# Splitting the last load and the first store of one DMA queue into unequal rows

**Chip, cores, metric.** One core of a Trainium2 chip. The metric is the device time of one execution in microseconds (us).

## The reference

Rotary position embedding with scaled positions, on x of shape (8, 8, 1024, 64) in fp32, 16.8 MB in and 16.8 MB out:

```python
angles = np.outer(positions * scale, freqs)          # (1024, 32)
cos, sin = np.cos(angles), np.sin(angles)
x_first, x_second = x[..., :32], x[..., 32:]
out = concatenate([x_first*cos - x_second*sin, x_first*sin + x_second*cos], -1)
```

## The kernel before

x is cut into four units of 4 MB, 128 partitions of 32 KB each. GpSimd's DMA queue loads the units and casts them to fp16 on the way (half of unit 0 comes as fp32 over the two other queues). VectorE does four products and sums a half unit, ScalarE casts the result back to fp32. Units 0 and 1 are stored by the same GpSimd queue, units 2 and 3 by SyncE's, a half unit at a time.

```python
N = 8192; NH = 4096; NU = 4                     # columns of a unit, of half a unit; units
X  = [xin.tile([P, K, 2, half], FP16, name=f"X{u}") for u in range(NU)]
pin(nc.gpsimd.dma_start(out=Xf[0][:, :NH], in_=xv[0][:, :NH]))
# ... constants on GpSimd ...
for u in range(1, NU):
    pin(nc.gpsimd.dma_start(out=Xf[u], in_=xv[u]))           # fp32 -> fp16
# ... sine and cosine tables (T) ...
for u in range(NU):
    OUT = xout.tile([P, N], FP32, tag="O")
    for s in range(2):
        # pr = X*sin; X = X*cos; X0 = X0 - pr1; X1 = pr0 + X1     (VectorE, half a unit)
        pin(nc.scalar.copy(out=OUT[:, ns], in_=Xf[u][:, ns]))
        if u >= NU // 2:
            pin(nc.sync.dma_start(out=ov[u][:, ns], in_=OUT[:, ns]))
    if u < NU // 2:
        pin(nc.gpsimd.dma_start(out=ov[u], in_=OUT))
```

`pin` keeps the program order on each engine. The queue of GpSimd therefore holds: units 0 to 3 in, unit 0 out, unit 1 out.

Of the kernel before, what the change touches and what calls it, by code (L numbers as in the profile page):

```python
# [21 lines left out]
def kernel(  # L22
# [8 lines left out]
    nc = tc.nc  # L31
    pin = tc.keep_in_program_order
# [8 lines left out]
    N = K * D  # L41
    NU = NBH // HEADS
# [2 lines left out]
    K8 = S // P  # L45
    G = P // HP
    W = K8 * half
    assert S % HP == 0 and D == 2 * half and NBH % HEADS == 0 and G * K8 == K

    fscale = float(scale)  # L50

    xv = x.rearrange("b h s d -> (b h s d)").rearrange("(u p n) -> u p n", p=P, n=N)
    ov = out.rearrange("b h s d -> (b h s d)").rearrange("(u p n) -> u p n", p=P, n=N)
# [21 lines left out]
    Xf = [t.rearrange("p k h j -> p (k h j)") for t in X]  # L75
# [12 lines left out]
        out=one, in_=one, compare_op=ALU.not_equal, fill=1.0, base=0,  # L88
        pattern=[[-1, G], [-G, HP]], channel_multiplier=1,
    ))  # L90
    for u in range(1, NU):
        pin(nc.gpsimd.dma_start(out=Xf[u], in_=xv[u]))  # L92


    pin(nc.vector.tensor_copy(out=sel, in_=one.unsqueeze(2).broadcast_to((P, G, HEADS, HP))))  # L95
# [5 lines left out]
        out=posf, in_=pos_i64.bitcast(I32).rearrange("p (k t) -> p k t", t=2)[:, :, 0]  # L101
# [3 lines left out]
        out=y,  # L105
# [8 lines left out]
        out=r, in0=m, scalar=_MAGIC, in1=y, op0=ALU.subtract, op1=ALU.subtract  # L114
# [5 lines left out]
        out=ra.bitcast(I32), in0=r.bitcast(I32), scalar1=0x7FFFFFFF, scalar2=None, op0=ALU.bitwise_and  # L120
# [5 lines left out]
    for g in range(0, G, 2):  # L126
        ps = spread.tile([P, 2, 2, W], FP32, tag="g")
        for i in range(2):
            nc.tensor.matmul(  # L129
                out=ps[:, i].rearrange("p t w -> p (t w)"),  # L130
# [12 lines left out]
# [3 lines that stand above are left out]
            ks = slice(s * KH, (s + 1) * KH)  # L146
            ns = slice(s * NH, (s + 1) * NH)
            Xs = X[u][:, ks]
            sin_b = T[:, 0, ks].unsqueeze(2).broadcast_to((P, KH, 2, half))
            cos_b = T[:, 1, ks].unsqueeze(2).broadcast_to((P, KH, 2, half))  # L150
            pr = tmp.tile([P, KH, 2, half], FP16, tag="pr")
            pin(nc.vector.tensor_tensor(out=pr, in0=Xs, in1=sin_b, op=ALU.mult))  # L152
            pin(nc.vector.tensor_tensor(out=Xs, in0=Xs, in1=cos_b, op=ALU.mult))  # L153
            pin(nc.vector.tensor_tensor(  # L154
                out=Xs[:, :, 0, :], in0=Xs[:, :, 0, :], in1=pr[:, :, 1, :], op=ALU.subtract
            ))
            pin(nc.vector.tensor_tensor(  # L157
                out=Xs[:, :, 1, :], in0=pr[:, :, 0, :], in1=Xs[:, :, 1, :], op=ALU.add
            ))
            pin(nc.scalar.copy(out=OUT[:, ns], in_=Xf[u][:, ns]))  # L160
            if u >= NU // 2:
                pin(nc.sync.dma_start(out=ov[u][:, ns], in_=OUT[:, ns]))
        if u < NU // 2:
            pin(nc.gpsimd.dma_start(out=ov[u], in_=OUT))  # L164


# [33 lines left out]
```

## Time and profile before

| | before |
|---|---|
| time, median of the runs given with the change | 84.56 us (84.42 to 84.83) |
| span in the profile | 82.8 us |
| HBM traffic over the span | 406 GB/s |
| VectorE / ScalarE busy | 73% / 49% |
| last ScalarE copy ends / last DMA packet ends | 73.4 / 81.5 us |

The last row is the one to start from: computing is over 8 us before the transfers are. The profile's own lines are shown in the prediction.

A word on how the text counts. Sixteen DMA engines share each transfer; each has 8 of the 128 rows. The profile records each row that an engine moves as a packet, with its start and duration; "packet records" below means these. From the start of one 32 KB row of fp32 to the start of the next, an engine takes 1.21 us, loaded or stored. Durations of single rows come out some 0.01 to 0.02 us longer.

### The profile page before, as it was taken

To read this page: it belongs to the slowest core of one execution; us is meant where nothing else is said; L and a number is where in the kernel's file an instruction comes from. 1 tells how busy PE (TensorE), PEld (TensorE's weight loads), DVE (VectorE), ACT (ScalarE), POOL (GpSimd) and SP (SyncE) were. 2 spreads that over 40 slices of the span, in tenths; PEclk is the share of its full clock that TensorE was granted. 3 is DMA by queue.
4 is the path that set the end of the run, shared out by engine and by line. 5 is a ranking of instruction groups with operands and counts; after the bars stand their busy time and mean duration, and the time that the engine had idled before them with its cause. 6 is when DMAs were issued, how large, how long until landed. Compare 5 with 4: busy or idle time off the path is not lost.

```text
span 82.8 us, 179 instructions
## 1 busy us (share of the span) xinstructions
PE 7.0 (8%) x18; PEld 2.7 (3%) x18; DVE 60.3 (73%) x40; ACT 40.1 (49%) x18; POOL 4.6 (6%) x14
## 2 busy tenths in 40 slices
PE   0011799200000000000000000000000000000000
PEld 0011233000000000000000000000000000000000
DVE  0306276999999999999999999999999997000000
ACT  0602159999960690294088049209606912950000
POOL 4920000000000002000000200000000000000000
PEclk9999999975555555555555555555555555555555
DMA  2899998997999899699979989999899999999991
GB/s 40 335 326 269 293 333 182 253 238 150 246 253 198 182 253 238 143 253 253 127 301 459 507 348 412 507 443 420 380 436 420 412 420 436 444 420 436 428 428 55
DMA packets 1874, 26.22 MB, mean 317 GB/s; under 512 B 338, under 2 KB 338, under 8 KB 338
## 3 DMA queue, kind: packets, MB, share of 16 engines
q0 software_dynamic: 864, 15.73, 66.4%
q1 hardware_dynamic: 720, 9.44, 27.2%
q10 hardware_dynamic: 290, 1.06, 3.2%
HBM read 16.79 MB, written 16.78 MB: 406 GB/s over the span
## 4 chain that ended last, share of the span: by engine, by line
DVE 55%; ACT 14%; issue 6%; DMA 6%; PE 5%; DVEq 1%; ACTq 0%
DVE pr L152 19%; DVE X L153 19%; DVE X L157 9%; DVE X L154 6%; DMA freq_row<-in_freqs_dram 6%; ACT T L139 5%; ACT OUT L160 4%; PE ps L129 4%; ACT X L140 4%; DVEq L195 1%; PE cfreq L97 1%; ACT tab L122 1%; DVE r L113 1%; DVE y L104 1%; ACTq L69 0%
## 5 line engine op out<-in xcount | busy, mean ns | idle before, releaser
L160 ACT CAST OUT<-X 128x4096 f32<-128x4096 f16 x8 | 28.8, 3606 | 24.2 <-DVE X L157 24.2
L152 DVE TENSOR_TENSOR pr<-X,T 128x4096 f16<-128x4096 f16 x8 | 18.3, 2292 | 1.0 <-ACT T L139 0.7
L153 DVE TENSOR_TENSOR X<-X,T 128x4096 f16<-128x4096 f16 x8 | 18.3, 2292 | 0.3
L154 DVE TENSOR_TENSOR X<-X,pr 128x2048 f16<-128x2048 f16 x8 | 9.8, 1225 | 0.3
L157 DVE TENSOR_TENSOR X<-pr,X 128x2048 f16<-128x2048 f16 x8 | 9.7, 1219 | 0.0
L139 ACT CAST T<-ps 128x1024 f16<-128x1024 f32 x6 | 5.7, 1030 | 2.6 <-PE ps L129 2.6
L129 PE MATMUL ps<-tab,sel 128*128 128x512 f16 x16 | 6.4, 584 | 2.2 <-ACT tab L122 2.2
L137 DVE CAST T<-ps 128x1024 f16<-128x1024 f32 x2 | 2.5, 1225 | 2.2 <-PE ps L129 2.2
L140 ACT CAST X<-X0f 128x4096 f16<-128x4096 f32 x1 | 3.7, 3651 | 0.0
L164 POOL DMA_DIRECT2D out_dram<-OUT x2 | 1.1, 536 | 40.3 <-ACT OUT L160 40.3
L95 DVE COPY sel<-one 128x2048 f16<-128x2048 f16 x1 | 0.7, 693 | 2.8 <-POOL one L87 2.8
L117 ACT ACTIVATE tab<-r 128x256 f16<-128x256 f32 x1 | 0.4, 416 | 4.3 <-DVE r L113 4.3
L129 PEld LDWEIGHTS <-sel 128*128 128x128 f16 x16 | 2.2, 138 | 6.0 <-issue 5.8
L117 ACT ACT_TABLE_LOAD x1 | 1.3, 1283 | 2.1 <-issue 2.1
L92 POOL DMA_DIRECT2D X<-in_x_dram x3 | 2.0, 658 | 0.0
L100 DVE CAST posf<-pos_i 128x8 f32<-128x8 int32 x1 | 0.2, 172 | 2.3 <-DMA pos_i<-in_positions_dram 2.3
L97 PE MATMUL cfreq<-freq_row,coef 1*128 1x32 f32 x2 | 0.6, 392 | 5.9 <-DMA freq_row<-in_freqs_dram 5.9
L104 DVE TENSOR_TENSOR y<-posf,cfreq 128x256 f32<-128x256 f32 x1 | 0.4, 422 | 0.5 <-PE cfreq L97 0.5
L83 POOL DMA_DIRECT2D X<-in_x_dram x1 | 0.7, 667 | 0.8 <-POOLq L181 0.8
L97 PEld LDWEIGHTS cfreq<-freq_row,coef 1*128 1x128 f32 x2 | 0.5, 305 | 5.8 <-issue 5.8
L122 ACT ACTIVATE tab<-ra,quarter 128x256 f16<-128x256 f32 x1 | 0.5, 507 | 0.0
L113 DVE SCALAR_TENSOR_TENSOR r<-m,y 128x256 f32<-128x256 f32 x1 | 0.4, 424 | 0.0
(10 smaller groups left out, 1.9 us busy)
## 6 DMA issues: line engine op xcount, KB each, us to landing
out_dram<-OUT POOLq DMA_DIRECT2D x2, 4096.0 KB, 20.8
out_dram<-OUT SPq DMA_DIRECT2D x4, 2048.0 KB, 11.6
X<-in_x_dram POOLq DMA_DIRECT2D x3, 2048.0 KB, 28.7
X0f<-in_x_dram SPq DMA_DIRECT2D x1, 1024.0 KB, 4.8
X<-in_x_dram POOLq DMA_DIRECT2D x1, 1024.0 KB, 11.7
X0f<-in_x_dram ACTq DMA_DIRECT2D x1, 1024.0 KB, 12.2
pos_i<-in_positions_dram ACTq DMA_DIRECT2D x1, 8.0 KB, 5.0
freq_row<-in_freqs_dram ACTq DMA_DIRECT2D x1, 0.1 KB
```

The source lines that it names most:

```text
L92: pin(nc.gpsimd.dma_start(out=Xf[u], in_=xv[u]))
L97: nc.tensor.matmul(out=cfreq, lhsT=coef, rhs=freq_row, start=True, stop=True)
L117: pin(nc.scalar.activation(out=tab[:, 0], in_=r, func=AF.Sin, bias=0.0, scale=-_TWO_PI_DN))
L129: nc.tensor.matmul(out=ps[:, i].rearrange("p t w -> p (t w)"), lhsT=sel[:, g + i].rearrange("s h q -> s (h q)"), rhs=tab.rearrange("s t k ...
L137: pin(nc.vector.tensor_copy(out=dst, in_=ps))
L139: pin(nc.scalar.copy(out=dst, in_=ps))
L140: pin(nc.scalar.copy(out=Xf[0][:, NH:], in_=X0f[:, :NH]))
L152: pin(nc.vector.tensor_tensor(out=pr, in0=Xs, in1=sin_b, op=ALU.mult))
L153: pin(nc.vector.tensor_tensor(out=Xs, in0=Xs, in1=cos_b, op=ALU.mult))
L154: pin(nc.vector.tensor_tensor(out=Xs[:, :, 0, :], in0=Xs[:, :, 0, :], in1=pr[:, :, 1, :], op=ALU.subtract))
L157: pin(nc.vector.tensor_tensor(out=Xs[:, :, 1, :], in0=pr[:, :, 0, :], in1=Xs[:, :, 1, :], op=ALU.add))
L160: pin(nc.scalar.copy(out=OUT[:, ns], in_=Xf[u][:, ns]))
```

## The change

Its intent: at the point where the queue of GpSimd goes from loads to stores, make the rows small, so that whatever is lost there is lost on small rows.

```diff
+    C1 = 512
+    C2 = 1024
...
     for u in range(1, NU):
-        pin(nc.gpsimd.dma_start(out=Xf[u], in_=xv[u]))
+        c = C2 if u == NU - 1 else 0
+        pin(nc.gpsimd.dma_start(out=Xf[u][:, : N - c], in_=xv[u][:, : N - c]))
+        if c:
+            pin(nc.gpsimd.dma_start(out=Xf[u][:, N - c :], in_=xv[u][:, N - c :]))
...
         if u < NU // 2:
-            pin(nc.gpsimd.dma_start(out=ov[u], in_=OUT))
+            c = C1 if u == 0 else 0
+            if c:
+                pin(nc.gpsimd.dma_start(out=ov[u][:, :c], in_=OUT[:, :c]))
+            pin(nc.gpsimd.dma_start(out=ov[u][:, c:], in_=OUT[:, c:]))
```

## The prediction

> **What bounds the kernel now.** I first asked whether an engine or the transfers bound it. The page's head and the slices answer, with the number of bytes:
>
> ```profile
> PE 7.0 (8%) x18; PEld 2.7 (3%) x18; DVE 60.3 (73%) x40; ACT 40.1 (49%) x18; POOL 4.6 (6%) x14
> ...
> DMA  2899998997999899699979989999899999999991
> ...
> HBM read 16.79 MB, written 16.78 MB: 406 GB/s over the span
> ```
>
> VectorE is busy 73% of the span and ScalarE 49%, while the DMA row is at 8 or 9 nearly everywhere (its single 6s and 7s come from packets being counted in the slice where they start; all sixteen engines step almost together). The second row of the page that matters is the chain, and it is a trap here: it is made of VectorE pieces and ends with the last ScalarE copy,
>
> ```profile
> 67.45 1.22 DVE X L154
> 68.67 1.15 DVEq L195
> 69.82 0.02 issue
> 69.84 3.60 ACT OUT L160
> ```
>
> that is at 73.44 us, but the span is 82.8 us. After it only the last 2 MB store is issued (73.47 us in the timeline). The packet records of the trace show that its packets don't start then: the last eight rounds of 16 KB packets on the SyncE queue start at 76.64 us and end at 81.50. So the last store waits some 3 us behind its own queue. The compute chain has those 3 us of slack, less the time from issue to a first packet (about 1 us for the first load of all, issued at 0.74, first packet at 1.75), so about 2 us. The bound is the sum of the transfers. Check: 33.57 MB at the 430 GB/s of the last stretch below is 78.1 us; from the first packet at 1.75 us that gives 79.8, and the packets end at 81.5. About 1.7 us are lost somewhere, and that is all that any re-cutting of transfers can win.
>
> Next I looked for where they are lost. I put the edges of windows on the starts of rounds of packets (one row a DMA engine, sixteen engines):
>
> ```profile
> core 0: us, PE busy (x) PEld busy (x) DVE busy (x) ACT busy (x) POOL busy (x), PEclk, DMA share, GB/s
> 21.88:31.57 9.69, 0.00 (x0) 0.00 (x0) 9.55 (x6) 5.74 (x2) 0.05 (x1) 0.50 1.02 216
> 31.57:38.82 7.25, 0.00 (x0) 0.00 (x0) 7.15 (x5) 3.61 (x1) 0.49 (x1) 0.50 1.02 217
> 38.82:42.03 3.21, 0.00 (x0) 0.00 (x0) 3.15 (x4) 0.38 (x1) 0.00 (x0) 0.50 1.06 163
> 42.03:51.73 9.70, 0.00 (x0) 0.00 (x0) 9.56 (x6) 6.26 (x2) 0.53 (x1) 0.50 1.00 433
> ...
> 66.29:80.88 14.59, 0.00 (x0) 0.00 (x0) 3.49 (x3) 3.76 (x2) 0.00 (x0) 0.50 1.00 430
> ```
>
> The last column counts bytes written, and a load casts fp32 to fp16, so 217 GB/s there is 434 GB/s read: loads and stores run at one pace, 32 KB of fp32 in 1.21 us an engine. Only the third line falls out: the last two rows of unit 3 (2 x 16 x 16 KB = 524 KB) take 3.21 us, where 217 GB/s would give 2.42. That is 0.8 us lost, with the engines busy all the time (share 1.06): the packets themselves are slow. Their records say so: every load row took 1.23 us; of the last two, the first took 1.23 to 1.71 us and the second 1.81 to 2.17. Taken on the engine that is last, from the end of its row before (39.25) to its first store packet (42.67), it is 3.43 - 2.42 = 1.0 us. Nothing like it shows between two loads (21.88 us) or two stores (51.73 us), where start to start is 1.23 and 1.21 us. It happens where the one queue of GpSimd turns from loads (unit 3) to stores (unit 0, issued at 31.52 us and waiting behind unit 3). The change is aimed at this spot.
>
> **What the Trainium skill says.** "DMA: Bandwidth & Descriptors", section "Two DMAs through the same engine are not ordered": descriptors of a queue start in order but are pipelined, and an engine's read and write sides are separate queues. So the read side can be at unit 0's store while the write side is still at unit 3's rows. The trace agrees in kind: the slow rows are the two before the first store, and nothing after. The same page, section "Specifications", gives about 435 GB/s as the ceiling of sixteen engines; measured here are 430 to 434. Its section "Where 436 GB/s comes from" says that for HBM to SBUF about 358 binds; the trace, with one core at work, does not show that. "Perfetto Trace Analysis", section "DMA Optimizations", warns of transfers under 2 KB and says that splitting helps if the DMA engines are idle; here they are not, so the gain can come from the turn alone.
>
> **The change, part by part.** Bytes are the same. Per DMA engine, unit 3 goes from 8 rows of 32 KB to 8 of 28 KB and then 8 of 4 KB (2 KB in fp16); unit 0's store from 8 of 32 KB to 8 of 2 KB and then 8 of 30 KB.
> - Added: 16 rows an engine. The cost of a row from the trace: start to start is 0.607 us for 16 KB and 1.209 for 32 KB, so 2 x 0.607 - 1.209 = 0.005 us a row; 16 x 0.005 = 0.08 us, on the path.
> - Added: two completion packets an engine, 0.02 us each where one follows a load (1.23 against 1.21 us start to start): 0.04 us at most, on the path.
> - Added: two issues on GpSimd of 0.54 us (the store's own duration; loads take 0.54 to 0.89). They lie beside other work: unit 3 is issued by about 5 us and its packets start at 31.58; the store is issued at 31.5 and its packets can't start before some 41 us.
> - Removed: some of the loss at the turn, which is 0.8 to 1.0 us. If the read side runs ahead by a fixed number of rows (two slow rows suggest one or two), what overlaps at the turn are rows of 4 KB and 2 KB instead of 32 KB. The loss scales with that, 1.0 x 4/32 = 0.13 us, and 0.87 is won. Less 0.12 of overhead: -0.75 us.
> - Compute: unit 3 is needed at 55.75 us and lands at 42.7; unit 0's buffer is needed again at 62.84 us and is stored by 52.4. Nothing there waits, before or after. Everything behind the turn on that queue moves up by what is won, and so does the last SyncE store, since its issue leaves about 2 us of room.
>
> **Rivals.**
> 1. The read side runs ahead by bytes, not by rows. 1.0 us at 27 GB/s an engine is 27 KB, and the two slow rows hold 64 KB of source. Then 8 small rows (16 KB of stores, 32 KB of loads) are swallowed and the next large row meets the same turn: nothing won, overhead paid, 84.5 + 0.1 = 84.6 us. For it: at 55.8 us the SyncE queue's first packets come some 2 us after they should be ready, about 32 to 64 KB behind the rows already taken in. Against it: two rows fits that as well. I give it 3 in 10.
> 2. The turn's loss is shared reading and writing of SBUF, for as long as it takes to turn; then it depends on the time the two overlap, and a part is won, perhaps half: 84.1 us.
> 3. The turn is won but the end does not move, because the last store becomes bound by its issue at 73.47 us. With some 2 us of room against 0.9 won, I don't believe it: 1 in 20.
> 4. Small rows cost much more than 5 ns, above all with a cast (4 KB to 2 KB). Even 50 ns a row would be 0.8 us and cancel the gain. The trace has no such row; its 8 KB rows of fp32 run at 0.31 us, at full pace. 1 in 10.
>
> **Range and chances.** Won 0.75 (about 5 in 10): 83.75. Half (2 in 10): 84.1. Nothing or a little worse (3 in 10): 84.5 to 84.7. The middle of these is 83.9 to 84.0; I take 83.9, since the two different sizes, 512 and 1024 elements, look searched for. The executions of before lie between 84.42 and 84.83, so the range is 83.5 to 84.7. Faster by over 2% needs 1.7 us, as much as all that is lost anywhere, twice the turn: 0.03. Slower by over 2%: the queue of GpSimd would have to stall, 0.02.
>
> **What would show it.** In the profile of after: rows of 4 KB near 41 us; the time from the last full-pace row of unit 3 to the first 30 KB row of unit 0, less bytes over 27 GB/s an engine, should fall from 1.0 to some 0.3 us; the last packet should end near 80.8 us instead of 81.5; the compute chain should stay where it is, with its last copy ending at 73.4. If rows of 28 KB or 30 KB beside the turn are now slow as well, rival 1 holds; if the small rows take much over 0.15 and 0.08 us each, all alike, rival 4. If the last packets follow the issue at 73.47 directly, rival 3. I am wrong altogether if the time moves by over 1.5 us.

## The result, and the profile after

84.41 us (84.34 to 84.51, 6 runs) against 84.56 us (84.42 to 84.83, 6 runs). The ratio is 0.9978, 95% interval 0.9958 to 0.9997. A ratio here is the mean time of one kernel's runs over the mean of the other's of the same rounds, so not quite the ratio of the medians quoted. I had forecast 0.62 us less (83.9 against 84.52, the median of the three runs known then); 0.15 us came.

First the page of the kernel after, the same three lines as before:

```profile
PE 6.4 (8%) x18; PEld 2.4 (3%) x18; DVE 60.3 (73%) x40; ACT 40.1 (49%) x18; POOL 5.7 (7%) x16
...
DMA  3899998996998999999499889989899899999991
...
HBM read 16.79 MB, written 16.78 MB: 406 GB/s over the span
```

Same work, two GpSimd instructions more, same rate over the span. (The 4 in the DMA row is the slice before many small packets start; packets count where they start.) GpSimd's timeline shows its first two stores, the small piece of unit 0 and the rest:

```profile
24.32 0.55 POOL L171 DMA_DIRECT2D out_dram<-OUT  x1 [19.13 <-ACT OUT L165]
31.54 0.53 POOL L172 DMA_DIRECT2D out_dram<-OUT  x1 [6.66 <-ACT OUT L165]
```

The small piece needs only the first half of unit 0's result, so it is in the queue 7.2 us before the rest; the prediction had 31.5 us for both. Its eight rows of 2 KB an engine are also not recorded as eight packets, but as four of 4 KB (64 in all), so the change adds 12 packets an engine and not the 16 rows of the prediction. The end of the chain of waits:

```profile
69.84 0.02 issue
69.86 3.60 ACT OUT L165
```

The compute chain did not move: last copy over at 73.46 us, before 73.44. Then the windows of the kernel after, with edges on its own rounds of packets: seven rows of 28 KB; the last such row with the 4 KB loads and the 2 KB stores; eight rows of 30 KB. The columns are those of the prediction's table (last: share of the DMA engines busy, GB/s written):

```profile
31.58:38.98 7.40, 0.00 (x0) 0.00 (x0) 7.30 (x5) 3.60 (x1) 0.49 (x1) 0.50 1.02 217
38.98:42.85 3.87, 0.00 (x0) 0.00 (x0) 3.80 (x4) 1.17 (x1) 0.00 (x0) 0.50 1.02 179
42.85:51.93 9.08, 0.00 (x0) 0.00 (x0) 8.94 (x6) 5.64 (x2) 0.53 (x1) 0.50 1.02 440
```

The middle line is the turn. At full pace it would take: 16 x (14 + 16) KB = 492 KB of fp16 at 217 GB/s, 2.26 us, and 262 KB of stores at 433 GB/s, 0.61 us; together 2.87. It took 3.87. The loss is 1.0 us, as large as before. The packet records show where it sits: full-pace rows of 28 KB took 1.08 us; the last took up to 2.24 us on some engines, on the others the first 4 KB row took up to 0.93 us (full pace is 0.17), and single later ones up to 0.58. The last 4 KB rows and all store rows run at full pace. So the slowness sits mostly between some 60 and 20 KB of source before the first store, and in sum it is as large as before, though rows there are small.

For comparing kernels I use one number from here on. **Turn loss**: the time from the completion of unit 2's load to the completion of unit 0's store, each the mean of the sixteen engines' completion packets, less 19.38 us (16 rows at full pace; one kernel below reaches exactly this). Before 20.36 - 19.38 = 0.98 us, after 20.42 - 19.38 = 1.04 us. Other profiled kernels in which the store waits early in the queue give 0.8 to 1.0, and one (warm_sp) 0.63, so differences of 0.1 to 0.2 mean nothing here.

### The profile page after: what moved, and what is told of

Its sections match the earlier page's. It is cut to its first block, busy times and chain, and to the rows that moved or that the text cites. A ratio compares the mean times of both kernels' runs of the same rounds, so it can differ in the third digit from the quotient of the medians.

```text
span 82.7 us, 184 instructions
## 1 busy us (share of the span) xinstructions
PE 6.4 (8%) x18; PEld 2.4 (3%) x18; DVE 60.3 (73%) x40; ACT 40.1 (49%) x18; POOL 5.7 (7%) x16
## 3 DMA queue, kind: packets, MB, share of 16 engines
q10 hardware_dynamic: 290, 1.06, 3.2%
## 4 chain that ended last, share of the span: by engine, by line
DVE 54%; ACT 14%; issue 7%; DMA 6%; PE 5%; DVEq 1%; ACTq 0%
DVE X L158 19%; DVE pr L157 19%; DVE X L162 9%; DMA freq_row<-in_freqs_dram 6%; ACT T L144 5%; DVE X L159 5%; ACT OUT L165 4%; PE ps L134 4%; ACT X L145 4%; DVEq L203 1%; PE cfreq L102 1%; ACT tab L127 1%; DVE r L118 1%; DVE y L109 1%; ACTq L71 0%
## 5 line engine op out<-in xcount | busy, mean ns | idle before, releaser
L134 PE MATMUL ps<-tab,sel 128*128 128x512 f16 x16 | 5.8, 503 | 2.6 <-ACT tab L127 2.2
L172 POOL DMA_DIRECT2D out_dram<-OUT x2 | 1.1, 531 | 20.2 <-ACT OUT L165 20.2
L95 POOL DMA_DIRECT2D X<-in_x_dram x3 | 2.0, 658 | 0.0
L171 POOL DMA_DIRECT2D out_dram<-OUT x1 | 0.6, 554 | 19.1 <-ACT OUT L165 19.1
L85 POOL DMA_DIRECT2D X<-in_x_dram x1 | 0.7, 669 | 0.8 <-POOLq L189 0.8
L97 POOL DMA_DIRECT2D X<-in_x_dram x1 | 0.6, 557 | 0.0
```

The costliest lines, as they stand in the source:

```text
L95: pin(nc.gpsimd.dma_start(out=Xf[u][:, : N - c], in_=xv[u][:, : N - c]))
L134: nc.tensor.matmul(out=ps[:, i].rearrange("p t w -> p (t w)"), lhsT=sel[:, g + i].rearrange("s h q -> s (h q)"), rhs=tab.rearrange("s t k ...
```

## The experiments

After the first result there were two questions: what is lost at the turn if not the rest of a row, and where the 0.15 us come from. Each run was made beside the kernel before, on the same chip.

### A ruler

```diff
-        pin(nc.gpsimd.dma_start(out=Xf[u], in_=xv[u]))
+        step = 1024 if u == NU - 1 else N
+        for c in range(0, N, step):
+            pin(nc.gpsimd.dma_start(out=Xf[u][:, c : c + step], in_=xv[u][:, c : c + step]))
```
and the same for the store of unit 0.

> A ruler, not a candidate: unit 3 is loaded and unit 0 stored in eight DMAs of 4 KB rows each, so that the place of the loss can be read to 4 KB. Bytes theory (the read side runs ahead by a fixed amount of data, so the size of rows at the turn doesn't matter): rows go slow for about 1.0 us in all, some 64 to 28 KB of source before the end of unit 3, and the last rows before the turn are back at full pace of about 0.155 us; time is that of before plus 112 rows at 0.005 us, 85.1 us. Rows theory (runs ahead by one or two rows; my prediction): slow are only the last one or two rows, the loss is under 0.2 us, 84.2 us.

Measured: 85.14 us against 84.52, ratio 1.0074 (1.0058 to 1.0089). Rows of 4 KB take 0.17 us up to 40.0 us; from there to 42.3 us, over the last eleven or so rows (44 KB of source), single rows on single engines take up to 0.66; the very last is at 0.17 again. A DMA of eight 4 KB rows took 1.253 us in the undisturbed part (six of them from 31.77 to 39.28), where one 32 KB row takes 1.209; so rows cost 0.006 us each with the completions, close to the 0.005 of the prediction. Loss by the definition: 1.14 us, of which 0.63 is rows (8 x 1.253 + 8 x 1.248 = 20.01 us at pace, against 19.38), leaving 0.5; the last two load DMAs took 1.46 and 1.55 us, which is the same 0.5. That is half, where I expected all of it to stay (bytes) or under 0.2 (rows). Neither fits cleanly: slowness begins well before one or two rows, but cutting all of both transfers does halve it, and costs more than that.

### Without the cast before the turn

```diff
+    pin(nc.gpsimd.dma_start(out=Xf[3][:, :6144], in_=xv[3][:, :6144]))   # cast
+    pin(nc.gpsimd.dma_start(out=Xq, in_=xv[3][:, 6144:]))                # plain fp32
...
+        if u == 2: pin(nc.scalar.copy(out=Xf[3][:, 6144:], in_=Xq))
```

> The last quarter of unit 3 (8 rows an engine of 8 KB, 64 KB of source) is loaded as plain fp32, without the cast, into a tile of its own, by the same queue, and ScalarE casts it later in its idle time. Theory cast: the loss belongs to going from rows that are cast (16 KB written for 32 KB read) to rows that are not. Then the slow packets move to the last 24 KB rows of the cast part, some 2 us earlier, and the plain rows run at 0.31 us up to the turn; time as before, 84.5 us. Theory memory: it belongs to the read side going from HBM to SBUF. Then the plain rows just before the turn are slow, by 1.0 us together, and the cast rows are all at pace; 84.5 us as well. If both are needed together, the loss is gone: 83.6 us.

Measured: 84.52 us against 84.52, ratio 0.9998 (0.9983 to 1.0013). All 24 KB cast rows took 0.93 us, at pace; of the 8 KB plain rows (0.31 us at pace) the third to the eighth took up to 0.74. Turn loss 0.86 us. The cast is not needed for it: slow are the last loads before the stores, cast or plain.

### The stores on a queue of their own

```diff
         if u < NU // 2:
-            pin(nc.gpsimd.dma_start(out=ov[u], in_=OUT))
+            pin(nc.sync.dma_start(out=ov[u], in_=OUT))
```

> The stores of units 0 and 1 are issued by SyncE, so they have a queue of their own and start at about 32 us among the loads of unit 3, instead of behind them. Theory head start (paid once, when the read side first gets ahead into stores): 1.0 us at most in all, 83.6 to 84.5 us. Theory per turn (each change from a load row to a store row of one engine costs 1 us): eight rows of unit 3 alternate with store rows, so 8 us and more, 92 us. If the reads of HBM and of SBUF can share the time of an engine, the alternating rows take less than 2.42 us a pair and it is faster than 83.6.

Measured: 85.06 us (84.76 to 85.51) against 84.52, ratio 1.0075 (1.0034 to 1.0116). Unit 3's second and third row took up to 1.55 and 2.48 us, just before the first store packets at 35.9 us; then load rows and store rows alternate at 2.43 us a pair, no slower than 2 x 1.21. From the start of the first load row to the start of the first store row it is 4.36 us (means over the engines), where three rows take 3.63: 0.7 us lost. So the loss came once, over 6 us earlier and with the store on another queue, and not again in the turns from row to row: "per turn" falls. In the profile the last packet ends at 81.5 us as before, but the span is 83.1 us instead of 82.8; I did not find out why the end takes longer.

### Three turns

```diff
+        q = NH if u == NU - 1 else N
+        pin(nc.gpsimd.dma_start(out=Xf[u][:, :q], in_=xv[u][:, :q]))
...
         if u < NU // 2:
             pin(nc.gpsimd.dma_start(out=ov[u], in_=OUT))
+        if u == 0:
+            pin(nc.gpsimd.dma_start(out=Xf[3][:, NH:], in_=xv[3][:, NH:]))
```

> The second half of unit 3 is issued on the GpSimd queue behind the store of unit 0 instead of before it, so the queue turns load, store, load, store. Theory head start (1.0 us is lost going to stores and got back when the read side returns to loads): the same 84.5 us, with store-to-load rows that look short by about 1 us. Theory per turn: load-to-store costs 1.0 us each time and the way back costs nothing or as much: 85.5 to 86.5 us.

Measured: 84.74 us against 84.52, ratio 1.0023 (1.0008 to 1.0038). Windows of this kernel: first four rows of unit 3's first half; its last four; unit 0's store; unit 3's second half:

```profile
31.56:34.00 2.44, 0.00 (x0) 0.00 (x0) 2.41 (x3) 0.00 (x0) 0.98 (x2) 0.50 1.05 218
34.00:37.26 3.26, 0.00 (x0) 0.00 (x0) 3.19 (x3) 2.70 (x1) 0.00 (x0) 0.50 1.10 168
37.26:46.95 9.69, 0.00 (x0) 0.00 (x0) 9.55 (x6) 4.51 (x2) 0.54 (x1) 0.50 1.00 429
46.95:51.80 4.85, 0.00 (x0) 0.00 (x0) 4.78 (x4) 3.15 (x1) 0.00 (x0) 0.50 1.00 208
```

The first turn loses as ever (168 instead of 218 GB/s for 64 KB of source a DMA engine). The second half unit, between two stores, takes 4.90 us by mean completions instead of 4.84: the way back costs nothing, and the second way from loads to stores costs 0.06 us. Unit 1's store, issued at 45.51 us, stood in the queue behind these loads too, so waiting behind loads does not cost every time. Both theories expected something else: no cost per turn, but nothing is given back either, since no row ran short. In this profile it is paid once.

### Is it the first store of the run?

"Once" suggested a cost of the first store as such. Four kernels make a tiny transfer (64 bytes a partition) at the start:

```diff
+    warm = consts.tile([P, 16], FP32)
+    pin(nc.vector.memset(warm, 0.0))
+    pin(nc.scalar.dma_start(out=ov[0][:, :16], in_=warm))       # warm_act; warm_sp on sync
+    # warm_scratch: out= a scratch tensor in HBM; warm_sbuf: out= another SBUF tile
```

> As before, but SyncE's first transfer is a tiny store: 64 bytes of zeros from each of 128 partitions to unit 0's place in the output, which the real store of unit 0 writes over later. Theory first store (what costs 1.0 us is the first store that an engine does in the whole run, once): the turn at 40 us runs at full pace, loss under 0.2 us; the 1 us is paid at the start instead, hidden in part before the first load packets at 1.75 us: 83.6 to 84.5 us. Theory head start (the read side gets ahead by some 27 KB of store data, once, and writes wait meanwhile): 64 bytes a row are too little to build it up, the turn still costs 1.0 us, 84.6 us.

> The same tiny store, issued first by ScalarE, ahead of the positions, so that SyncE's load of unit 0 starts as before. Theory first store: no loss at the turn; 83.5 to 84.5 us, by how much of the 1 us the start hides. Theory head start: 84.5 us, and 1.0 us lost at the turn.

> The same tiny transfer, but from SBUF to SBUF: the read side reads SBUF early, and nothing is written to HBM. If warm_act takes the loss away and this doesn't, the cost belongs to the first write to HBM; if both do, to the first read of SBUF; if neither does, head start stands, 84.5 us.

> The same tiny store into a scratch tensor in HBM instead of the output. If the first-store cost is bound to the place that is written (the output's own addresses), the turn still costs 1.0 us here, 84.5 us; if to storing as such, it is gone as in warm_act. Under head start the turn costs 1.0 us in any case.

| | us | before | ratio (95%) | turn loss |
|---|---|---|---|---|
| warm_sp | 85.49 | 84.60 | 1.0104 (1.0083 to 1.0126) | 0.63 |
| warm_act | 85.08 | 84.60 | 1.0052 (1.0031 to 1.0073) | 0.81 |
| warm_scratch | 84.87 | 84.60 | 1.0029 (1.0010 to 1.0048) | 0.91 |
| warm_sbuf | 91.79 | 84.60 | 1.0823 (1.0770 to 1.0877) | 0.27 |

The three early stores to HBM do not take the loss away: last load rows up to 1.98, 2.18 and 2.21 us, and 0.63 to 0.91 us lost, where the theory "first store" had under 0.2. It falls. The 0.63 of warm_sp is low, and stays unexplained. In these three, as in sp_store, the span goes on for 1.6 to 1.7 us after the last packet, in the kernel before for 1.3; not followed up.

warm_sbuf is a failed experiment that gave the decisive hint. It is 7 us slower because the positions, behind the SBUF transfer on ScalarE's queue, came late: VectorE waited 9.0 us for them, and the whole compute chain came some 9 us later. But its turn is clean: the last load rows all took 1.23 us. Since its computing was late, its store of unit 0 was issued at 40.55 us, 1.1 us before its first packet, and not at 31.5. So either the SBUF transfer had paid the loss, or **the store was no longer waiting in the queue while the last loads were under way**.

### Issuing the store later

The rows stay whole. GpSimd copies one element a partition of a VectorE result before it issues the store of unit 0, so the issue waits for that result. Nothing else is changed.

```diff
     for u ...: for s ...:
         pr = X * sin                                                   # VectorE
+        if u == 1 and s == 1:
+            pin(nc.gpsimd.tensor_copy(out=gate, in_=pr[:, 0, 0, 0:1]))
+            pin(nc.gpsimd.dma_start(out=ov[0], in_=OUT0))              # late_37
         X = X * cos                              # late_39: gate behind this one
         X0 = X0 - pr1                            # late_40: behind this one
...
-        if u < NU // 2:
+        if 0 < u < NU // 2:
             pin(nc.gpsimd.dma_start(out=ov[u], in_=OUT))
```

> Rows and bytes as before; only the store of unit 0 is issued later: GpSimd first copies one element a partition of the product that VectorE ends at 36.9 us, so the store is issued at about 37.2 us instead of 31.5. Loads of unit 3 end at 41.4 us if nothing slows them. Theory queue ahead (the loss arises because the store stands in the queue while the last 64 KB of loads are under way; in warm_sbuf it was issued at 40.55 us, 1.1 us before its first packet, and the turn lost only 0.2 to 0.3 us): here it is still early enough to be read ahead, loss 1.0 us, 84.5 us. Rival, once: the loss belongs to the first store whenever it comes, and warm_sbuf lacked it because its early SBUF to SBUF transfer had paid it: 1.0 us here and in the two others.

> The same, behind the product that ends at 39.2 us: issued at about 39.5 us, packets ready about 40.6, some 0.8 us before the loads end. Queue ahead: part of the loss, 0.3 to 0.7 us, 83.9 to 84.2 us. Once: 1.0 us, 84.5.

> The same, behind the subtraction that ends at 40.5 us: issued at about 40.7 us, packets ready at about 41.8, that is just after the loads end at 41.4. Queue ahead: last load rows at full pace (1.23 us), a gap of 0.2 to 0.5 us before the first store packet, 0.3 to 0.5 us lost instead of 1.0, 83.9 to 84.1 us. Once: the loss of 1.0 us remains and the gap comes on top, 84.6 to 85.0 us.

| | store issued at, us | us | before | ratio (95%) | turn loss |
|---|---|---|---|---|---|
| late_37 | 39.01 | **83.41** | 84.66 | 0.9853 (0.9840 to 0.9867) | 0.00 |
| late_39 | 40.33 | 83.79 | 84.66 | 0.9891 (0.9874 to 0.9909) | 0.27 |
| late_40 | 41.23 | 84.88 | 84.66 | 1.0029 (1.0013 to 1.0044) | 1.09 |

One of the eleven executions of the kernel before beside these was slow (86.33 us); the ratios leave it out. All three were issued later than I expected, because the copy itself waited: in late_37 it took 2.31 us, as long as the VectorE product beside it (2.29 us). The Trainium skill, "SBUF — State Buffer", section "SBUF: two separate sides", says that a VectorE operation with two SBUF inputs and a GpSimd operation that reads SBUF exclude each other for the whole instruction; this trace agrees. So late_37's expectation, that it would still be too early, rested on a wrong issue time, and late_39 and late_40 were too late.

Windows of late_37: six rows of unit 3; its last two; unit 0's store:

```profile
31.54:38.81 7.27, 0.00 (x0) 0.00 (x0) 7.17 (x5) 3.60 (x1) 2.05 (x1) 0.50 1.02 216
38.81:41.23 2.42, 0.00 (x0) 0.00 (x0) 2.39 (x3) 0.00 (x0) 0.74 (x2) 0.50 1.02 217
41.23:50.92 9.69, 0.00 (x0) 0.00 (x0) 9.46 (x7) 5.97 (x2) 0.53 (x1) 0.50 1.00 433
```

The middle line now has the 2.42 us that the prediction worked out as full pace (kernel before: 3.21 us and 163 GB/s), and the store starts without a gap. The sixteen engines' last packets end at 80.18 us in the mean and 80.41 at the latest; in the kernel before at 81.22 and 81.50.

In late_40 the loads are as clean, but then the engines stand still. Windows: last two rows of unit 3; the gap; the store:

```profile
38.90:41.33 2.43, 0.00 (x0) 0.00 (x0) 2.40 (x3) 0.05 (x1) 1.16 (x2) 0.50 0.98 209
41.33:42.34 1.01, 0.00 (x0) 0.00 (x0) 1.01 (x1) 1.01 (x1) 0.44 (x1) 0.50 0.09 32
42.34:52.17 9.83, 0.00 (x0) 0.00 (x0) 9.69 (x6) 6.15 (x2) 0.53 (x1) 0.50 1.00 427
```

And the stores behind the gap are slower: 427 instead of 433 GB/s, rows of 1.21 to 1.30 us by the packet records, in late_39 too (up to 1.32). A queue that is filled just in time has no such slow rows in late_37. In late_39 the gap is 0.1 us by the means (loads done at 41.37, stores from 41.51). The time of late_40 alone would fit the rival "once" (the first store costs 1.0 us whenever it comes; 84.6 to 85.0 us), and its gap is twice what I expected; but its load rows are clean, so what it loses is the gap. "Once" falls in all three; "queue ahead" holds.

### The moment, or the gate?

late_37 differs from before in the copy as well as in the moment. Two kernels have the copy, placed half a unit earlier:

> As late_37, with the gate one half unit earlier, behind the subtraction of unit 1's first half: issued at about 34.6 us, 6.8 us before unit 3's loads can end (41.4). Theory reads in flight (the read side is some 64 KB, 2.4 us, ahead of the write side; if store descriptors are there when it runs out of load rows at about 39.0 us, it takes 27 KB of store data in while those loads still come, and they arrive 1.0 us late; if they come later, nothing is lost): ready at some 35.6, long before 39.0, so 1.0 us is lost as before, 84.6 us. Rival, the gate: it is GpSimd's copy, not the moment, that helped late_37: no loss here either, 83.4 us.

> The same behind the addition of unit 1's first half: issued at about 36.9 us, ready at about 38, still before 39.0. Reads in flight: the loss is whole or nearly so, 84.2 to 84.6 us. If it fades evenly between an issue at 31.5 (1.0 us) and at 39.0 (none): 0.3 us lost, 83.7 us. The gate: 83.4 us.

Measured: late_35 84.50 us against 84.57, ratio 0.9987 (0.9963 to 1.0011), turn loss 0.85 us, issued at 34.68. late_36 84.60 us, ratio 1.0002 (0.9972 to 1.0031), turn loss 1.00 us. GpSimd's timeline of late_36 and then of late_37 (start, duration, instruction):

```profile
34.65 2.31 POOL L163 COPY gate<-X 128x1 f16<-128x1 f16 x1 [29.97 <-DVE X L158]
36.89 0.54 POOL L164 DMA_DIRECT2D out_dram<-OUT  x1
```

```profile
36.76 2.31 POOL L156 COPY gate<-pr 128x1 f16<-128x1 f16 x1 [32.11 <-DVE pr L153]
39.01 0.54 POOL L157 DMA_DIRECT2D out_dram<-OUT  x1
```

The same copy of the same length, 2.12 us apart. And the turn of late_36, same kind of windows as late_37's:

```profile
31.56:38.82 7.26, 0.00 (x0) 0.00 (x0) 7.16 (x5) 3.61 (x1) 2.79 (x2) 0.50 1.02 217
38.82:42.13 3.31, 0.00 (x0) 0.00 (x0) 3.24 (x4) 0.47 (x1) 0.00 (x0) 0.50 1.07 168
42.13:51.82 9.69, 0.00 (x0) 0.00 (x0) 9.55 (x6) 6.25 (x2) 0.53 (x1) 0.50 1.00 429
```

So it is the moment. Issued at 31.5, 34.7 or 36.9 us the store costs the loads 0.85 to 1.0 us; at 39.0, 2.4 us before the loads' end, it costs nothing. It does not fade evenly; between 36.9 and 39.0 us there is a step or a steep fall.

### The change's rows on top of the late store, and each half of the change

late_split is late_37 with the change's C1 and C2. load_only and store_only are the change's two halves; after_again is the changed kernel once more.

> late_37 with the change's own splits on top. If the turn is clean because the store comes late, the small rows have nothing to win: 16 rows at 0.005 us, three more completions and one more issue before the large store cost 0.1 to 0.2 us, and the 2 KB rows may not bridge the time to the large store's descriptors (0.54 us later): 83.5 to 83.9 us. If small rows help on their own account, under 83.3 us.

> The first half of the change alone: unit 3 in rows of 28 and then 4 KB, unit 0 stored whole. Reads in flight: 1.0 us lost at the turn as in both kernels, time 84.4 to 84.7 us. Rows theory of the prediction (lost is what one or two rows hold): small load rows before a large store row should win about half, 84.0 us.

> The second half of the change alone: unit 3 loaded whole, unit 0 stored in rows of 2 and then 30 KB. Reads in flight: 1.0 us lost as in both kernels, plus 0.05 us for the rows; 84.4 to 84.7 us. If the small gain of the change (ratio 0.9978) comes from this half, the ratio is 0.998 or lower here; if the gain is chance, 1.000.

> The changed kernel once more, beside store_only and the kernel before on one chip: if its small gain is real, the ratio is 0.996 to 0.999 again; the mean of the engines' last packets should be no earlier than before's (81.22 us), with the ends closer together (0.4 us instead of 0.6). If it was chance, the ratio is 1.000 and the spread is not smaller.

| | us | before | ratio (95%) | turn loss | last packets of the 16 engines, us |
|---|---|---|---|---|---|
| late_split | 83.60 | 84.57 | 0.9880 (0.9857 to 0.9903) | 0.07 | 80.09 to 80.60 |
| load_only | 84.48 | 84.57 | 0.9987 (0.9959 to 1.0015) | 0.96 | 81.00 to 81.41 |
| store_only | 84.50 | 84.56 | 0.9987 (0.9965 to 1.0010) | 0.96 | 80.93 to 81.54 |
| after_again | 84.44 | 84.56 | 0.9982 (0.9961 to 1.0003) | 0.93 | 81.08 to 81.37 |
| change (first result) | 84.41 | 84.56 | 0.9978 (0.9958 to 0.9997) | 1.04 | 81.06 to 81.45 |
| before | | | | 0.98 | 80.89 to 81.50 |

With the loss gone, the small rows win nothing: 83.60 us, while late_37 had 83.41 (other rounds; ratios 0.9880 and 0.9853). late_37 is the fastest version found, faster than both kernels, by 1.5% against the one before.

No half of the change shows a gain clear of noise, and the repeat's interval just includes 1. What the profiles show is that the *mean* of the engines' last packets is not earlier with the change (81.27 and 81.23, before 81.22), only the *latest* is (81.45 and 81.37, before 81.50), since the engines end 0.3 to 0.4 us apart instead of 0.6. The 4 KB load rows seem to draw them together (load_only 0.4, store_only 0.6). That is one profile each and a matter of 0.1 us: a likely source of the 0.15 us, not a shown one.

## Why the prediction was right or wrong

- **The bound: right.** The sum of transfers sets the time. Where the last packets came 1.09 us earlier (late_37), the time fell by 1.25 us, and the compute chain did not become the bound.
- **Where and how much is lost: right.** 0.8 to 1.0 us, on the last 64 KB before the turn; late_37 shows that this much was there to be had.
- **Added rows and completions, +0.12 us: small, as forecast, and rather less.** The ruler gives 0.006 us a row with its completions, but 12 packets an engine came and not 16. With the loss away the turn of late_split is 0.07 us longer than late_37's (one profile each); in the change the mean of the last packets came 0.05 and 0.01 us later.
- **Removed, -0.87 us: this is the step that failed.** I took the loss to be what one or two rows hold, and scaled it by 4 KB over 32 KB. Measured were 1.04 and 0.93 us lost with the small rows, against 0.98: nothing removed. The ruler contradicts the count of rows as well: its slow rows are spread over the last eleven, not one or two. What counts is how long before the end of the loads the store is in the queue. That the slow rows were two of two I had read as a number of rows; it was a stretch of 64 KB, or 2.4 us, which happened to be two rows.
- **The likelihoods.** I gave 5 in 10 to the step that failed and 3 in 10 to rival 1, which has the outcome right (nothing won) but puts it 0.2 us too high. Its bytes are half right: the ruler still loses 0.5 us where all rows are 4 KB. Rival 2 (reading and writing share SBUF at the turn) does not fit late_37, where loads and stores meet in the same way without loss; rival 3 does not fit it either, since its end moved with the turn; rival 4 falls with the 4 KB rows, 0.17 us each at pace. The range held the result; the centre, 83.9, was off by 0.5 us. The chances as written give a mean of 84.1, not 83.9 to 84.0, and rivals 1, 3 and 4 together have 4.5 in 10, not the 3 in 10 that "nothing" was given; that the sizes look searched for is no evidence from a profile.
- **A question I did not ask** was whether the store's early issue could harm. I noted that it waits from 31.5 to 41 us and took this as harmless.

What the runs show: the first large store, when it is in the queue while the last 64 KB of loads before it are moved, costs these loads 0.5 us (the ruler) to 1.0 us, once in the run; one that is issued 2.4 us before their end costs nothing; one that is issued 1.1 us or less before their end leaves a gap (0.1 us in late_39, 1.0 in late_40). It came without the cast too (0.86 us), with the store on another queue (0.7) and after an earlier small store (0.63 to 0.91). Each of these losses is read from one profile. An explanation that fits and is only argued: the read side of a DMA engine works ahead of its write side by some 64 KB of loads; when it finds store rows there, it takes some 27 KB of them in (1.0 us at 27 GB/s) while the last loads are still to come, and those arrive that much later. The write side can't use the early data faster than 1.21 us a row, so the time is not made up; and since the lead persists, the second turn of three_turns costs nothing. That the ruler loses only half would need more than this.

## What to carry to other kernels

When transfers are the bound, look for the stretch where packets are slow, not only where engines are idle; here the busy share there was 1.06 while 25% of the pace was missing. Where a store waits in a queue behind loads with nothing to gain from waiting, try issuing it later, timed to some two microseconds before the loads end, and check from both sides, since too late costs as well: issued 2.2 us after late_37's, the store of late_40 lost all that late_37 had won (84.88 us). Before sizing a gain by a unit (a row), change the unit in an experiment: that the loss covers two rows does not say that it is counted in rows.

## What the Trainium skill lacked or had wrong

- "DMA: Bandwidth & Descriptors", section "Two DMAs through the same engine are not ordered", has the pipelining of read and write sides but not its price: a store queued behind loads slowed the last 64 KB of them by 1.0 us a DMA engine (0.85 to 1.0 when issued at 34.7 or 36.9 us, none at 39.0).
- The same page, section "Rules for kernel authors", advises to issue a DMA early so that its setup overlaps with computing, and has no word of a case against it. Here the earlier issue was the slower: 84.60 us (issued at 36.9) and 83.41 us (39.0), in runs beside a kernel of 84.57 and 84.66 us.
- The same page, section "Where 436 GB/s comes from", says that about 358 GB/s binds between HBM and SBUF, in that sentence without saying for how many working cores. With one core at work 434 GB/s were loaded over 7 us and 430 to 433 stored over 10 and 15 us.
- No page has that a queue filled too late runs slower afterwards: 427 GB/s (late_40, behind a gap of 1.0 us) and 426 (late_39, 0.1 us) instead of 433.
